# A two-layer encoder on one core: when banks are read, zeros behind the first transposes, where the last chunks are scaled, and who sums the MLP's weights

## The chip, the cores and the metric

The kernel runs on one core of one Trainium2 chip. The metric is the device time of one execution in microseconds (us). TensorE (PE) multiplies and writes PSUM banks; VectorE (DVE) and ScalarE (ACT) read those banks and work on tiles in SBUF; GpSimd (POOL) and SyncE (SP) issue the DMAs. PEld is PE's loading of weights, which overlaps its products.

## The reference

```python
for l in range(DEPTH):                       # 2 layers, x: 512 tokens by 1024
    h = _rmsnorm(x, g_mix[l])
    x = x + _mixer(h, l, w_in[l], ...)       # three attentions, three gates, one output projection
    h = _rmsnorm(x, g_mlp[l])
    x = x + jnp.square(jax.nn.relu(h @ w_up[l])) @ w_down[l]    # 1024 -> 4096 -> 1024
return _rmsnorm(x, g_final)
```

Inside the mixer one attention is dilated: a query sees keys of a window, and the scores of the group with dilation 1 are masked, their maximum is subtracted, and they are exponentiated.

## The kernel before

Everything is float32. A product is made of three matmuls: each operand is split into a high part (ACT copies it rounded) and a low part (DVE subtracts the high part from the original), and high times high, high times low and low times high are summed in a PSUM bank. Activations stand with features on the partitions and the 512 tokens along the row.

**A plan in place of written order.** Each line of the kernel only records an operation (`record`, line 184). `record` finds what it must wait for: for each tile read, the earlier writes that touch the same region (line 212), and for each tile written, earlier reads and writes. `schedule` (line 318) then walks through a model of time. Each engine takes, of the operations that are ready, the one recorded first (`key`), if its tiles fit in the slots; `cost` (line 247) gives durations, `bank_free` (line 473) keeps a bank from two engines at once, `try_alloc` (line 392) gives out tiles, and the DMA queues of POOL and SP are held to a backlog. At most 12 tiles `w` (cut weights) and 6 tiles `raw` (loaded weights) are alive, which sets how far the cutting can run ahead of the products. `emit` (line 598) writes the instructions out in the planned order, all from line 607, so that the profile shows L607 for nearly all of them; the tile names tell them apart. On the chip each engine runs its own list in order.

**The start** (from line 671). PE multiplies a tile of zeros six times (`warm`) while x is loaded. Then PE transposes x in eight blocks `k` of four 128x128 pieces into banks `x0` (shown as `x`), and DVE and ACT split each into `h`. The first products `mm<-w,h` follow.

**Scores** (`dil_scores`, line 1340). For the first group, two halves `i` of a bank `sp` (tile `s`) get two matmuls each, and then DVE reads each half with the mask, and writes `p0` (tile `pd`) and its maximum (`sm`):

```python
sp = P("s", [128, 2, 256])
for i in range(2):
    ten.matmul(sp[:, i], ..., kk[:, 0, w], start=True, stop=False)
    ten.matmul(sp[:, i], ..., kk[:, 1, w], start=False, stop=True)
for i in range(2):
    dve.tensor_tensor_reduce(p0[:, c], sp[:, i], mask0[...], ..., accum_out=ml0[:, c, 0:1])
```

There are four such units in a layer, of two banks each.

**The MLP** (label `mlp`). Nine of 16 pairs of up blocks (`up_pair`, line 1703, the numbers in `UP`) and all down blocks but the last (`down`, line 1743) use seven products in place of eight, in the way of Strassen and Winograd. `weights` (line 1668) loads four quarters a11, a21, a12, a22 of a weight block and makes seven cut operands of them, four of which are sums: s1 = a21 + a22, s2 = s1 - a11, a21 - a11, and a12 - s2 (tile `ss`, 128x512, or 128x384 where a group has three pairs). A set of these operands feeds 84 matmuls of 256 columns (63 with three pairs). There are 25 sets in a layer. Groups of 3, 4, 4 and 3 pairs (`PAIRS`) run one after the other: first the ups of the group, then its four downs, whose seven products `keep` (line 1754) adds up over the groups in DRAM by DMAs `da<-da` on POOL's queue, and `outputs` (line 1781) puts together at the end of the last group. On POOL the DMAs `da` each wait for ACT's copy of a bank. The seven products of a down block lie by pairs in banks (`BANKS`).

The last two pairs of ups, 14 and 15, have no Strassen form. Their squares `b` are split into `u` (`hilo`), multiplied with the last rows of w_down, and the result in the bank is multiplied by R2, the square of the norm's factor per token, into a tile `t`, and added to x (`xt`). In the last layer the columns 768 to 1023 are done in two halves of the tokens, then squared, summed and normed, transposed and written out.

Of the kernel before, what the change touches and what calls it, by code (L numbers as in the profile page):

```python
# [101 lines left out]
class Plan:  # L102
# [81 lines left out]
    def record(self, eng, m, args, kw):  # L184
# [23 lines left out]
        for v in reads:  # L208
            r = self.region(v)
            b = v.buf  # L210
            for w, wr in b.writes:
                if hit(wr, r):
                    preds.add(w.i)
            b.reads.append((op, r))
            if b not in op.bufs:
                op.bufs.append(b)
# [30 lines left out]
    def cost(self, eng, m, args, kw, reads, writes):  # L247
# [7 lines left out]
        if "dma" in m:  # L255
# [31 lines left out]
            return 900 if eng == "gpsimd" else 475 if k <= 256 else 600, lat  # L287
        n = free(o)
        psum = any(isinstance(v, View) and v.buf.space == "P" for v in reads)
        if m == "transpose":  # L290
# [27 lines left out]
    def schedule(self):  # L318
# [73 lines left out]
        def try_alloc(op):  # L392
# [19 lines left out]
            for b in new:  # L412
                if op.eng == "gpsimd" and o["lifo"]:

# [62 lines left out]
        while nleft:  # L477
# [9 lines left out]
            for e in engs:  # L487
                pe_, av_ = pend[e], avail[e]
                while pe_ and pe_[0][0] <= t:
                    i = heapq.heappop(pe_)[1]  # L490
                    heapq.heappush(av_, (ops[i].key, i))
                if free_t[e] > t or not av_ or e == "gpsimd" and flow_left() > o["backlog"]:
                    continue
                skipped = []
                pick = None
                while av_ and len(skipped) < 40:
                    c = heapq.heappop(av_)
                    w = bank_free(ops[c[1]])
                    if w > t:
                        heapq.heappush(pe_, (w, c[1]))  # L500
                        continue
                    if try_alloc(ops[c[1]]):
                        pick = ops[c[1]]
                        break
                    skipped.append(c)
# [12 lines left out]
                for b in op.bufs:  # L518
                    if b.users[-1] is op and b.words > 8 and b.cls:
                        u = [x for x in b.users if not done[x.i]]  # L520
                        if u:
# [3 lines left out]
                            if u[-1].i not in alloc_seen(evs, u[-1].i):  # L525
                                bisect.insort(evs, u[-1].i)
                if e in dmaq:
                    inq += op.lat
# [92 lines left out]
def trunk(ctx, tc, x, w_in, b_gate, g_mix, diff_lambda, g_diff, g_cq, g_ckv, w_uq, w_ukv,  # L621
# [6 lines left out]
    dr = ctx.enter_context(tc.tile_pool(name="dr", bufs=1, space=DRAM))  # L628
    opts = dict(n2=12, n4=42, limits=dict(x0=8, mm=5, s=3, tp=2, av=2, raw=6, w=12, p=8, pd=4, pt=4), boost=20, vecs=14e3, warm=6, backlog=6000, slack=150, late=120, dmalat=-750, dslack=3000, entry=300, begin=dict(gpsimd=1075, sync=560), lifo=1, ahead=dict(xt=300, raw=350, tb=300))
    plan = Plan(nc, sb, ps, x, {8: 64, 512: opts["n2"], 1024: opts["n4"]}, opts)  # L630
# [42 lines left out]
    dve.memset(zero, 0.0)  # L673
    p = P("mm")
    for _ in range(opts["warm"]):
        ten.matmul(p[:, :128], zero[:, :128], zero[:, :128], start=True, stop=True)
    mark("")
# [166 lines left out]
    for k in range(KD):  # L844
# [3 lines left out]
        norm.split(k, p)  # L848
        ps0.append(p)
    plan.boost = -opts["late"]  # L850
    for k in range(0, KD, 2):
# [35 lines left out]
    def layer(l, norm):  # L887
# [780 lines left out]
        def weights(w, k0, n, c0):  # L1668
# [15 lines left out]
            p1 = cut(a11)  # L1684
            s1 = add(dve.tensor_add, a21, a22)
            s2 = add(dve.tensor_sub, s1, a11)
            p6 = cut(s2)
            p7 = cut(add(dve.tensor_sub, a21, a11))
            p5 = cut(s1)
# [124 lines left out]
        for n in range(first, 16):  # L1814
            b = up_pair(n)
            for i in range(2):
                u = H("u")
                hilo(u, b[:, i].rearrange("p t n -> p (t n)"))
                us.append(u)
# [8 lines left out]
        for mp in range(4):  # L1828
# [6 lines left out]
            for i in range(2):  # L1835
                m = 2 * mp + i
                t = T("t")
                dve.tensor_mul(t, pp[i], R2)
                dve.tensor_add(xt[m], xt[m], t)
                if last:  # L1840
# [12 lines left out]
        for hh in range(2):  # L1853
# [5 lines left out]
            for i in range(2):  # L1859
                xm = xt[6 + i][:, cs]  # L1860
                t = T("t")
                dve.tensor_mul(t[:, cs], pp[i], R2[:, cs])
                dve.tensor_add(xm, xm, t[:, cs])
                sq = T("t")
# [81 lines left out]
```

## Time and profile before

| | us |
|---|---|
| median of 3 runs | 1913.08 (1911.11 to 1913.43) |
| the profiled execution | 1911.94 |
| its span in the trace | 1910.1 |
| PE busy | 1884.4 (99%) |
| DVE busy | 1547.6 (81%) |
| ACT busy | 1050.9 (55%) |
| POOL busy | 138.3 (7%) |

PE is at work nearly always, so the profile is read by PE's waits and by what stands ahead of them on the engine that ends them. The busy shares are averages over stages: in the attention of either layer DVE is busy for 71 to 87% of the time, in the first two thirds of the MLP for over 90%.

### The profile page before, as it was taken

How to read it: one execution, taken by the hardware profiler on the slowest of the kernel's cores; microseconds unless marked ns; L12 is line 12 of the kernel's file. 1: busy time of each engine (PE TensorE's matmuls, PEld its weight loads, DVE VectorE, ACT ScalarE, POOL GpSimd, SP SyncE). 2: the span in 40 equal slices, each digit the busy share in tenths (PEclk: the TensorE clock that was granted, in tenths of full speed). 3: DMA queues.
4: the chain of work that ended last, by engine and by line, in shares of the span. 5: the costliest groups of instructions: out<-in, count | busy, mean ns of one | idle time of the engine just before them, and what ended most of it. 6: DMA issues, size and time to landing. Idle time of an engine off the chain costs nothing.

```text
span 1910.1 us, 31918 instructions
## 1 busy us (share of the span) xinstructions
PE 1884.4 (99%) x11908; PEld 1685.5 (88%) x11908; DVE 1547.6 (81%) x3347; ACT 1050.9 (55%) x2029; POOL 138.3 (7%) x174
## 2 busy tenths in 40 slices
PE   9999999999999999999999999999999999999998
PEld 8888888887888999999988888888877889999997
DVE  7788867787788998958867988687877789989496
ACT  5564645544345776755444755455434467677544
POOL 0000001100110001010100000011001100010000
PEclk9999999999999999999999999999999999999999
DMA  8934636667562457592557364366766535384741
GB/s 221 235 100 129 187 116 187 175 166 228 155 176 79 130 169 162 137 268 91 165 125 196 84 201 143 111 166 174 185 188 174 160 102 183 108 201 120 218 144 50
DMA packets 273844, 301.33 MB, mean 158 GB/s; under 512 B 99789, under 2 KB 218573, under 8 KB 273689
## 3 DMA queue, kind: packets, MB, share of 16 engines
q1 hardware_dynamic: 250136, 214.74, 39.6%
q0 software_dynamic: 23552, 84.55, 16.5%
q8 instruction: 94, 1.54, 0.3%
q14 instruction: 62, 0.50, 0.1%
HBM read 222.36 MB, written 72.69 MB: 154 GB/s over the span
## 4 chain that ended last, share of the span: by engine, by line
PE 79%; DVE 10%; issue 6%; ACT 2%; DMA 2%; SPq 0%; POOL 0%; DVEq 0%; ACTq 0%; POOLq 0%
PE mm L607 53%; PE x L607 15%; PE s L607 4%; PE tp L607 4%; PE av L607 3%; DVE w L607 3%; ACT w L607 1%; DVE da L607 1%; DVE hb L607 1%; DVE ss L607 1%; DVE sm L607 1%; DVE t L607 1%; DVE ht L607 1%; DMA dk<-rx 1%; DMA ml<-sm 1%
## 5 line engine op out<-in xcount | busy, mean ns | idle before, releaser
L607 PE MATMUL mm<-h,w 128*128 128x512 f32 x2400 | 604.9, 397 | 2.0 <-DVE w L607 2.0
L607 PEld LDWEIGHTS mm<-h,w 128*128 128x128 f32 x2400 | 439.8, 188 | 94.5 <-DVE w L607 3.2
L607 PE MATMUL x<-u,w 128*128 128x256 f32 x3864 | 461.4, 281 | 4.7 <-ACT w L607 3.1
L607 PEld LDWEIGHTS x<-u,w 128*128 128x128 f32 x3864 | 458.1, 189 | 7.7 <-ACT w L607 3.7
L607 DVE TENSOR_TENSOR w<-raw,w 128x512 fp32r<-128x512 f32 (+3 forms) x432 | 356.3, 841 | 65.3 <-ACT w L607 63.7
L607 ACT ACTIVATE w<-raw 128x512 fp32r<-128x512 f32 (+3 forms) x432 | 309.8, 749 | 35.2 <-PE x L607 10.3
L607 PE MATMUL mm<-u,w 128*128 128x256 f32 (+1 forms) x1560 | 206.0, 294 | 0.1
L607 PEld LDWEIGHTS mm<-u,w 128*128 128x128 f32 x1560 | 197.3, 189 | 7.8 <-ACT w L607 0.5
L607 PE MATMUL mm<-w,h 128*128 128x256 f32 (+1 forms) x1152 | 153.5, 286 | 0.0
L607 PEld LDWEIGHTS mm<-w,h 128*128 128x128 f32 x1152 | 147.3, 190 | 2.4 <-DVE w L607 0.2
L607 ACT ACTIVATE w<-ss 128x512 fp32r<-128x512 f32 (+1 forms) x200 | 114.8, 592 | 58.7 <-DVE ss L607 40.0
L607 DVE TENSOR_TENSOR w<-ss,w 128x512 fp32r<-128x512 f32 (+1 forms) x200 | 125.1, 646 | 13.3 <-ACT w L607 12.8
L607 POOL DMA_DIRECT2D raw<-in_w_in_dram x80 | 70.1, 878 | 883.4 <-PE mm L607 236.9
L607 ACT ACTIVATE p<-s,sm 128x512 f32<-128x512 f32 x128 | 87.3, 684 | 84.7 <-DVE sm L607 83.8
L607 PE MATMUL s<-qk,qk 96*128 96x512 f32 (+2 forms) x448 | 120.7, 365 | 4.3 <-DVE sm L607 4.3
L607 PE MATMUL mm<-co,w 128*128 128x512 f32 x456 | 114.4, 398 | 0.1
L607 ACT ACTIVATE pt<-tp 128x512 fp32r<-128x512 f32 x128 | 70.9, 595 | 70.1 <-PE tp L607 69.1
L607 DVE TENSOR_REDUCE sm<-s 128x1 f32<-128x512 f32 x128 | 85.5, 682 | 21.0 <-PE s L607 20.8
L607 PEld LDWEIGHTS mm<-co,w 128*128 128x128 f32 x456 | 83.9, 188 | 19.0 <-DVE co L607 0.5
L607 DVE TENSOR_TENSOR t<-mm,const 128x512 f32<-128x512 f32 (+1 forms) x98 | 64.3, 674 | 43.7 <-PE mm L607 43.6
L607 PE MATMUL mm<-om,w 128*128 128x512 f32 x384 | 99.4, 396 | 0.0
L607 PEld LDWEIGHTS s<-qk,qk 128*128 128x128 f32 (+1 forms) x448 | 79.4, 189 | 19.1 <-DVE sm L607 5.2
(164 smaller groups left out, 2330.2 us busy)
## 6 DMA issues: line engine op xcount, KB each, us to landing
raw<-in_w_in_dram POOLq DMA_DIRECT2D x77, 512.0 KB, 7.2
raw<-in_w_up_dram SPq DMA_DIRECT2D x64, 512.0 KB, 5.7
dk<-rx SPq DMA_DIRECT2D x40, 512.0 KB, 6.4
qk<-dk SPq DMA_DIRECT2D x40, 512.0 KB, 5.4
raw<-in_w_down_dram SPq DMA_DIRECT2D x32, 512.0 KB, 4.4
raw<-in_w_in_dram SPq DMA_DIRECT2D x27, 512.0 KB, 9.9
raw<-in_w_down_dram SPq DMA_DIRECT2D x32, 384.0 KB, 3.9
da<-da POOLq DMA_DIRECT2D x24, 512.0 KB, 7.3
```

The source lines that it names most:

```text
L607: getattr(getattr(self.nc, op.eng), op.m)(*args, **kw)
```

## The change

- `record`: a read of a PSUM bank waits for every write recorded for that bank so far, not only for those that touch what is read.
- `weights`: the sums a21 + a22 and a21 - a11 are made by POOL, and recorded ahead of the other two. `cost` has a duration for such a POOL operation, and `try_alloc`, the backlog and the entry into the queue apply to POOL's DMAs alone.
- The start: eight zeros in place of six, and twelve more behind the transposes of the second block, with a piece of x as the weights, into the bank `idle` that nothing reads.
- The last two ups: `b` is multiplied by R2 before it is split, and the products are added to x straight from the bank, in the three places where a multiplication by R2 stood.

```diff
-                if hit(wr, r):
+                if hit(wr, r) or b.space == "P":
                     preds.add(w.i)
...
+        if eng == "gpsimd":
+            return 2.1 * n + 200, 300
...
-                if op.eng == "gpsimd" and o["lifo"]:
+                if op.eng == "gpsimd" and o["lifo"] and "dma" in op.m:
...
-                if free_t[e] > t or not av_ or e == "gpsimd" and flow_left() > o["backlog"]:
+                if free_t[e] > t or not av_:
                     continue
+                full = e == "gpsimd" and flow_left() > o["backlog"]
...
+                    if full and "dma" in ops[c[1]].m:
+                        skipped.append(c)
+                        continue
...
-                if e in dmaq:
+                if "dma" in op.m:
...
-    p = P("mm")
-    for _ in range(opts["warm"]):
-        ten.matmul(p[:, :128], zero[:, :128], zero[:, :128], start=True, stop=True)
+    idle = P("mm")
+
+    def zeros(n, w):
+        for _ in range(n):
+            ten.matmul(idle[:, :128], w, zero[:, :128], start=True, stop=True)
+    zeros(opts["warm"], zero[:, :128])
...
+        if k == 1:
+            zeros(opts["fill"], xin[0][:, 0, :128])
...
-            s1 = add(dve.tensor_add, a21, a22)
+            s1 = add(plan.gpsimd.tensor_add, a21, a22)
+            s3 = add(plan.gpsimd.tensor_sub, a21, a11)
             s2 = add(dve.tensor_sub, s1, a11)
             p6 = cut(s2)
-            p7 = cut(add(dve.tensor_sub, a21, a11))
+            p7 = cut(s3)
...
-                u = H("u")
-                hilo(u, b[:, i].rearrange("p t n -> p (t n)"))
+                u, t = H("u"), b[:, i].rearrange("p t n -> p (t n)")
+                dve.tensor_mul(t, t, R2)
+                hilo(u, t)
...
-                t = T("t")
-                dve.tensor_mul(t, pp[i], R2)
-                dve.tensor_add(xt[m], xt[m], t)
+                dve.tensor_add(xt[m], xt[m], pp[i])
```

(In the options, `warm` is 8 in place of 6, and `fill=12` is new. In the last layer's half columns the same replacement stands as in the last hunk.)

On PE the order is the same in both kernels from the end of the start to the scores of a dilated unit in layer 0 (at 465 us in the trace). There the bank of scores (`s_5424`, in the changed kernel `s_5438`) gets its four products among those of a gate (`mm_5385`, `mm_5399`). Before:

```order
L607 MATMUL s_5424<-qk_5272,qk_5241 128x256
L607 MATMUL mm_5385<-h_312,w_5139 128x512
L607 MATMUL s_5424<-qk_5272,qk_5241 128x256
L607 MATMUL mm_5385<-h_312,w_5152 128x512
L607 MATMUL s_5424<-qk_5272,qk_5241 128x256
L607 MATMUL mm_5385<-h_338,w_5139 128x512 x2
L607 MATMUL mm_5385<-h_338,w_5152 128x512
L607 MATMUL s_5424<-qk_5272,qk_5241 128x256
L607 MATMUL mm_5385<-h_347,w_5139 128x512 x2
```

Now:

```order
L613 MATMUL s_5438<-qk_5286,qk_5255 128x256
L613 MATMUL mm_5399<-h_326,w_5153 128x512
L613 MATMUL s_5438<-qk_5286,qk_5255 128x256
L613 MATMUL mm_5399<-h_326,w_5166 128x512
L613 MATMUL s_5438<-qk_5286,qk_5255 128x256
L613 MATMUL mm_5399<-h_352,w_5153 128x512
L613 MATMUL s_5438<-qk_5286,qk_5255 128x256
L613 MATMUL mm_5399<-h_352,w_5153 128x512
L613 MATMUL mm_5399<-h_352,w_5166 128x512
```

The fourth product `s` has moved up by two matmuls; in layer 1 the same row moves in the same way. DVE's reads of that bank stand at the same place in its list.

On DVE, at the end of the last group's downs in layer 0, the sums `ss` stand between the additions of `keep` (`da<-da,x`) and `outputs` (`hb`, `da<-da`), which end the downs, and the cuts `w` of the next set. Before:

```order
L607 TENSOR_TENSOR ss_10590<-raw_10343,raw_10353 128x384
L607 TENSOR_TENSOR da_9981<-da_9981,x_2015_10519 128x512
L607 TENSOR_TENSOR da_9981<-da_9981,x_2016_10522 128x256
L607 TENSOR_TENSOR hb_10610<-da_9927,da_9981 128x256 x2
L607 TENSOR_TENSOR hb_10610<-da_9927 128x256
L607 TENSOR_TENSOR da_9927<-da_9927 128x256
L607 TENSOR_TENSOR ss_10624<-ss_10590,raw_10343 128x384
L607 TENSOR_TENSOR hb_10610<-da_9927,da_9981 128x256
L607 TENSOR_TENSOR ss_10629<-raw_10343 128x384
L607 TENSOR_TENSOR w_10627<-ss_10624,w_10627 128x384
L607 TENSOR_TENSOR w_10598<-ss_10590,w_10598 128x384
```

Now:

```order
L613 TENSOR_TENSOR ss_10614<-ss_10433,raw_10357 128x384
L613 TENSOR_TENSOR da_9979<-da_9979,x_2017_10537 128x512
L613 TENSOR_TENSOR da_9979<-da_9979,x_2018_10540 128x256
L613 TENSOR_TENSOR hb_10634<-da_9927,da_9979 128x256 x2
L613 TENSOR_TENSOR hb_10634<-da_9927 128x256
L613 TENSOR_TENSOR da_9927<-da_9927 128x256
L613 TENSOR_TENSOR w_10622<-ss_10614,w_10622 128x384
L613 TENSOR_TENSOR hb_10634<-da_9927,da_9979 128x256
L613 TENSOR_TENSOR w_10501<-ss_10411,w_10501 128x384
L613 TENSOR_TENSOR w_10508<-ss_10433,w_10508 128x384
```

The sum of a21 and a22 (`ss<-raw,raw`) and the difference a21 - a11 (`ss<-raw`) have left DVE, and s2 (`ss<-ss,raw`) stands ahead of the additions.

On POOL, in the downs of the first group, nothing but the DMAs `da` stood before:

```order
L607 DMA da_1024_116<-da_7365 128x1024
L607 DMA da_768_117<-da_7339 128x768
L607 DMA da_1024_118<-da_7404 128x1024
L607 DMA da_768_119<-da_7450 128x768
L607 DMA da_1024_120<-da_7496 128x1024
L607 DMA da_768_121<-da_7561 128x768
```

Now:

```order
L613 DMA da_1024_116<-da_7370 128x1024
L613 DMA da_768_117<-da_7352 128x768
L613 TENSOR_TENSOR ss_7430<-raw_7343 128x512
L613 DMA da_1024_118<-da_7412 128x1024
L613 TENSOR_TENSOR ss_7481<-raw_7343,raw_7394 128x512
L613 DMA da_768_119<-da_7466 128x768
L613 TENSOR_TENSOR ss_7543<-raw_7440 128x512
L613 DMA da_1024_120<-da_7512 128x1024
L613 DMA da_768_121<-da_7577 128x768
L613 TENSOR_TENSOR ss_7612<-raw_7440,raw_7518 128x512
```

The sums for the next sets stand between the DMAs `da`, two to a set. From the second group on the list goes on in this way.

## Rows read from the trace of the kernel before

**Rows 1.** The page, part 1: busy us (share of the span) xinstructions by engine.
```profile
PE 1884.4 (99%) x11908; PEld 1685.5 (88%) x11908; DVE 1547.6 (81%) x3347; ACT 1050.9 (55%) x2029; POOL 138.3 (7%) x174
```

**Rows 2.** PE's waits in the whole run: us in total, times, longest.
```profile
PE s L607 <- DVE sm L607: 4.3, 2, 2.2
PE x L607 <- ACT w L607: 3.1, 3, 1.3
...
PE tp L607 <- DVE pd L607: 1.3, 1, 1.3
PE x L607 <- DVE w L607: 0.8, 2, 0.4
...
PE x L607 <- DVE u L607: 0.5, 2, 0.3
```

**Rows 3.** Timeline: start, us, engine, line, op, out<-in, xcount [idle before <-releaser].
```profile
466.46 1.22 DVE L607 TENSOR_TENSOR w<-raw,w 128x1024 fp32r<-128x1024 f32 x1
...
467.67 0.42 DVE L607 CUSTOM_DVE_ANT_0 pd<-s,const 128x256 f32<-128x256 f32 x1
...
468.15 0.39 PE L607 MATMUL s<-qk,qk 128*128 128x256 f32 x1 [2.14 <-DVE sm L607]
...
468.38 6.41 PE L607 MATMUL mm<-h,w 128*128 128x512 f32 x27
```

**Rows 4.** Windows, layer 0: busy PE, PEld, DVE, ACT, POOL; then `ss`: DVE, ACT.
```profile
640.00:665.00 25.00, 25.00 (x214) 24.86 (x213) 24.94 (x61) 17.39 (x33) 1.13 (x3) 1.00 0.39 119
665.00:725.00 60.00, 59.42 (x501) 58.99 (x500) 57.80 (x102) 45.21 (x86) 3.23 (x6) 1.00 0.47 153
725.00:760.00 35.00, 34.93 (x296) 34.94 (x297) 28.67 (x48) 22.91 (x42) 6.04 (x7) 1.00 0.88 195
760.00:815.00 55.00, 55.00 (x469) 54.89 (x469) 54.70 (x94) 41.31 (x75) 1.80 (x3) 1.00 0.56 145
...
640.00:665.00 25.00, 12.24 (x24) 4.36 (x9) 1.00 0.39 119
665.00:725.00 60.00, 28.15 (x45) 13.96 (x25) 1.00 0.47 153
725.00:760.00 35.00, 20.98 (x33) 9.47 (x16) 1.00 0.88 195
760.00:815.00 55.00, 24.21 (x38) 12.10 (x21) 1.00 0.56 145
```

**Rows 5.** Timeline of PE at the start.
```profile
1.49 2.93 PE L607 MATMUL mm<-t 128*128 128x128 f32 x12 [1.49 <-DVE t L607]
5.98 1.94 PE L607 MATMUL x<-const,v 128*128 128x128 f32 x8 [1.56 <-DMA v<-in_x_dram]
9.11 1.97 PE L607 MATMUL x<-const,v 128*128 128x128 f32 x8 [1.19 <-DMA v<-in_x_dram]
10.73 4.43 PE L607 MATMUL mm<-w,h 128*128 128x288 f32 x20
14.99 1.03 PE L607 MATMUL x<-const,v 128*128 128x128 f32 x8
```

**Rows 6.** DVE's sums of weights by form: xcount | busy us, mean ns | idle before.
```profile
L607 DVE TENSOR_TENSOR ss<-raw,raw 128x512 f32<-128x512 f32 x34 | 23.4, 688 | 0.0
...
L607 DVE TENSOR_TENSOR ss<-raw,raw 128x384 f32<-128x384 f32 x16 | 8.8, 553 | 0.0
```

**Rows 7.** Timeline of DVE at the end, and of PE at the layers' border.
```profile
1899.81 0.41 DVE L607 TENSOR_TENSOR t<-mm,const 128x256 f32<-128x256 f32 x1
...
972.76 0.43 PE L607 MATMUL tp<-const,const 128*128 128x128 f32 x2 [0.44 <-DVE const L607]
```

**Rows 8.** POOL: one form of instruction; timeline of POOL and DVE at 732 us.
```profile
masks.py:199 POOL TENSOR_SCALAR_AFFINE_SELECT const<-const 128x128 f32<-128x128 f32 x1 | 0.3, 287 | 0.1
...
732.22 1.78 POOL L607 DMA_DIRECT2D da<-da  x2 [50.04 <-ACT da L607]
...
733.23 1.29 DVE L607 TENSOR_TENSOR w<-ss,w 128x512 fp32r<-128x512 f32 x2 [1.07 <-ACT w L607]
```

More of the change, by code (lines that the diff above doesn't have):

```diff
@@ L628, in trunk @@
     dr = ctx.enter_context(tc.tile_pool(name="dr", bufs=1, space=DRAM))
-    opts = dict(n2=12, n4=42, limits=dict(x0=8, mm=5, s=3, tp=2, av=2, raw=6, w=12, p=8, pd=4, pt=4), boost=20, vecs=14e3, warm=6, backlog=6000, slack=150, late=120, dmalat=-750, dslack=3000, entry=300, begin=dict(gpsimd=1075, sync=560), lifo=1, ahead=dict(xt=300, raw=350, tb=300))
+    opts = dict(n2=12, n4=42, limits=dict(x0=8, mm=5, s=3, tp=2, av=2, raw=6, w=12, p=8, pd=4, pt=4), boost=20, vecs=14e3, warm=8, fill=12, backlog=6000, slack=150, late=120, dmalat=-750, dslack=3000, entry=300, begin=dict(gpsimd=1075, sync=560), lifo=1, ahead=dict(xt=300, raw=350, tb=300))
     plan = Plan(nc, sb, ps, x, {8: 64, 512: opts["n2"], 1024: opts["n4"]}, opts)
@@ L1860, in layer @@
                 xm = xt[6 + i][:, cs]
-                t = T("t")
-                dve.tensor_mul(t[:, cs], pp[i], R2[:, cs])
-                dve.tensor_add(xm, xm, t[:, cs])
+                dve.tensor_add(xm, xm, pp[i])
                 sq = T("t")
```

## The prediction

> **What bounds the kernel now.** I read the page's busy times first: TensorE (PE) is busy for 1884.4 of 1910.1 us [rows 1]. No edit here takes a product away (the zeros add some), so nothing can be won but PE's waits and the two ends, some 25 us together. The second view is the list of what PE waited for [rows 2]. Its longest entry is 4.3 us in two waits of a matmul `s` for VectorE (DVE). The waits of `x` products, those of the MLP, for freshly cut weights or halves come to 3.1 + 0.8 + 0.5 = 4.4 us. The third view is the stall at 465 us, one of the two [rows 3]. PE writes the two halves of a bank of scores with four products `s`, and DVE may read half 0 as soon as the first two are done. That read (467.67) stands in DVE's queue behind a weight cut of 1.22 us (466.46), and PE's fourth product waits 2.14 us for it, since both touch one bank. The fourth view is the layer 0 MLP by stretches [rows 4]. In 640-665, 665-725 and 760-815 us DVE is busy for 24.94 of 25, 57.80 of 60 and 54.70 of 55 us while PE hardly waits; only 725-760 leaves it 6.3 us. So in the MLP DVE runs level with PE, and each microsecond put on DVE there is paid by PE.
>
> **Banks read whole.** In `record` a read of a bank now follows every product written to it so far. Only in the first loop of `dil_scores` are a bank's halves read one by one, so nothing else can move, and up to the MLP the order confirms it: apart from the start, one row moves in each layer, the fourth `s` product, two matmuls up. DVE's place for the reads stays. What PE waited for is gone, because the read is now behind the product. What is late next: 27 products `mm` follow the stall without a wait [rows 3], on weights cut before it. Gain 4.3 us, both layers. Cost: the read of half 0 now waits for two products more, but it starts 2 us behind them anyway: nothing. Bounds 2.2 (one stall comes back elsewhere) to 4.3; I take 4.3, the row itself.
>
> **Zeros at the start.** PE waits for x until 5.98 us, again until 9.11 [rows 5]. Eight transposes take 1.94 us there and 1.03 at 14.99, so the early ones run at the lower of the clock's two levels, though the column PEclk has no sign of it. Two more zeros in front end before 5.98: free. Twelve zeros between the first and the second block take twice the records of the first row each, 24 by 2.93/12 = 5.9 us at the lower level, half of it at the higher. They start at about 7.7. At the lower level throughout they end at 13.6; then come the transposes of 9.11, 1.0 us at the higher level, and the first 20 products, some 2.6 (a little over half of their 4.43, since the last of them ran fast already): 17.2 instead of 15.2, 2.0 lost. At the higher level from their start, they end at 10.6, and 1.0 and 2.6 more make 14.2: 0.9 won. Which it is depends on when the clock rises, and that no row of before tells. I take 0.5 lost, nearer to the middle.
>
> **Last chunks scaled first.** Removed: eight multiplications `t<-mm` per layer; added: four in SBUF on `b`, 0.69 us each like other rows of that shape [rows 6]. On the path to the end stands one: DVE multiplies for 0.41 us at 1899.81, adds behind it, and ScalarE (ACT) squares behind that [rows 7]. The sum goes straight from the bank now, so the end comes 0.4 us sooner; where the other `t<-mm` of 0.41 counts too, 0.8. At the layers' border the chain to the norm loses a multiplication of 0.69, and PE's wait of 0.44 there [rows 7] can go: 0.4. On the other side, the new multiplication stands between the square and the split of the last up pair, 0.7 us on a chain that ends shortly before PE needs it: 0.1 lost, cover DVE idle there. Together 0.7 won.
>
> **Two sums by GpSimd (POOL).** 25 sets of weights per layer, two sums each: DVE loses 34 + 16 rows of either kind, 0.688 or 0.553 us [rows 6]; two of 0.69 in a row take 1.29 (733.23, rows 8), so 0.60 is what one gives back, in the small form 0.46. POOL gets 100 sums. It has no tensor sum before; the nearest row that reads SBUF is a select over 128 elements, 0.287 us [rows 8], so a sum of 512 takes up to 1.15 us, of 384 up to 0.86 (an estimate). POOL is 93% idle, and one set feeds 84 products, 84 by 60/501 us = 10 us of PE [rows 4], so its own length is covered by a set's lead. POOL's queue is in order: sums now stand between the DMAs `da`, which wait for ACT (732.22, rows 8). A sum behind such a DMA waits with it; behind the sum wait DVE's second sum (and all that DVE has queued behind that) and ACT's cuts, and then PE. The set's lead of 10 us is the cover; where it is used up, PE waits for what is left of the `da` wait.
>
> The price that decides is what DVE loses while POOL reads SBUF beside it. The rows bound it from 0 to the whole sum, 1.15. For 0 speaks that DVE's cuts keep 0.69 while POOL issues DMAs for 1.78 us (733.23 beside 732.22, rows 8); but such an issue reads no tile, so that is the nearest row, not a near one. At 0 DVE is 0.60 ahead per sum, and nearly all of the 4.4 us of `x` waits go [rows 2], the longest two of 1.3 too: there DVE's second sum stood behind additions for the outputs, and in the new order stands ahead of them. I put 4.0 on it. At 0.60 the sum is even and nothing is won. I take the middle of these two, 2.0 won: some of the sums must fall beside DVE's reads of PSUM or its waits for ACT, and up to 0.6 of 1.15 costs nothing.
>
> The Trainium skill speaks against this edit. "SBUF — State Buffer", section "Who interferes with whom", states that a VectorE instruction with two inputs in SBUF contends with a GpSimd instruction that reads SBUF, and that whichever issues second stands still until the other is done. No row here shows such a pair. By that rule the whole sum would be lost, and the time would be that of the first rival below.
>
> **Sum**, against the profiled execution of 1911.94 us (span 1910.1): 4.3 won, 0.5 lost, 0.7 won, 2.0 won = 6.5 won: 1905.4. The median of the runs is 1.1 above that execution, by which it is 1906.6; I say 1906. With all bounds, the forecast's own range is 4.3 + 0.9 + 1.2 + 4.0 = 10.4 won to 4.3 - 2.0 + 0.7 = 3.0 won: 1901 to 1910.
>
> **Rivals.** *POOL's sums hold DVE* (slower). Each sum costs DVE 1.15 and gives back 0.60 (0.86 and 0.46). The sets in a stretch are the instructions on `ss` by eight [rows 4]: six small sums in 640-665, 11 in 665-725, 8 in 725-760, 9.5 in 760-815. Over DVE's idle time that is 6 by 0.40 = 2.4; 11 by 0.55 less 2.2 = 3.9; 8 by 0.55 less 6.3 = nothing; 9.5 by 0.55 less 0.3 = 4.9. So PE loses 11.2 us per layer, 22.4 in all, against 4.5 won elsewhere: 1913.1 + 17.9 = 1931. It decides from about 0.87 us lost per sum, where 11 by 0.27 - 2.2, 9.5 by 0.27 - 0.3 and 6 by 0.19 come to 4.2 per layer, and the whole is 3.8 slower. For it: DVE's instructions there nearly all read two tiles. Against it: DVE's waits for ACT and its PSUM reads take part of a sum.
>
> *The gain moves on* (same). The stalls of `s` go, but one of them comes back at the next late chain, `tp` waiting for `pd` (1.3 us already [rows 2]), whose DMAs need not move with PE; the zeros cost their 2.0, POOL's sums come out even: 4.3 - 2.2 - 2.0 + 0.7 = 0.8 won: 1912. This is also the case in which the first edit doesn't do what it says.
>
> **How the numbers follow.** 0.2% (3.8 us) is about what a measurement of this kernel can tell from no change. Forecast 0.52, of it 0.04 within 0.2%; POOL holds DVE 0.30, of it 0.04 within; moved gain 0.18, of it 0.03 faster, 0.01 slower. So faster 0.51, same 0.22, slower 0.27. The range reaches from the forecast's best, 1901, into the first rival, to 1925: about 0.05 is left out below, 0.12 above, the full price of that rival among it.
>
> **What would show it.** No wait of `s` for DVE in PE's list: the first step. PE's first 20 products starting before 12 us or after 14: the zeros. `xt<-xt,mm` directly ahead of the last square, and the end 0.4 us nearer: the scaling. POOL's sums at about 1.1 us, and DVE's cuts beside them at 0.69: the forecast; cuts of over 1 us and PE waits for `w` in the MLP of more than 5 us per layer: the first rival. I am wrong if DVE's instructions stretch beside POOL's sums by more than 0.6 each, or if the sums come late behind the `da` DMAs.

## The result, and the profile after

The changed kernel takes 1959.92 us (median of 4 runs, 1955.38 to 1960.51) against 1912.09 us before in the same session: a ratio of 1.0237, with an interval from 1.0225 to 1.025. I had forecast 1906 and a range of 1901 to 1925. It is 47.8 us slower (43 to 48 by the interval), beyond the full price that I gave to the first rival.

Part 1 of the page of the changed kernel:

```profile
PE 1907.9 (97%) x11936; PEld 1703.6 (87%) x11936; DVE 1575.1 (80%) x3237; ACT 1049.5 (54%) x2029; POOL 317.1 (16%) x274
```

Against [rows 1], DVE has 110 instructions fewer and is busy 27.5 us longer. So its other instructions got longer. POOL is busy for 178.8 us more, with 100 instructions more. PE has 28 more (14 zeros, two records each), and is busy 23.5 us longer; 24.3 us more of the span (50.0 instead of 25.7) is idle. The loss has these two halves.

PE's waits in the whole run of the changed kernel (us in total, times, longest):

```profile
PE x L613 <- DVE u L613: 15.2, 10, 3.2
PE x L613 <- ACT u L613: 12.5, 14, 2.5
PE tp L613 <- DVE sm L613: 5.0, 3, 2.5
PE x L613 <- DVE w L613: 3.8, 7, 0.9
```

The entry `s` for DVE, the longest of [rows 2], is gone, as the first step wanted. New are 27.7 us of waits of the MLP's products for `u`, the split halves. Weights `w`, which the first rival named, are only 3.8. New as well are two waits of `tp` for `sm` of 2.46 and 2.36 us (at 647.68 and 1613.28 us), in the norm ahead of the MLP: there DVE's small instructions on `sm`, 0.16 us alone, take up to 0.98 us beside a sum.

In the list of all waits of the changed kernel, none of PE, DVE or ACT is put down to a sum by POOL. The sums a21 + a22, taken in order, are done 1.1 us or more before DVE takes them up, in the median 11 us. So the sums do not come late.

The layer 0 MLP by stretches (us; busy PE, PEld, DVE, ACT, POOL with counts; granted clock, DMA share, GB/s):

```profile
640.00:665.00 25.00, 22.30 (x173) 21.70 (x172) 22.95 (x49) 14.93 (x28) 5.57 (x6) 0.93 0.30 88
665.00:725.00 60.00, 59.06 (x494) 58.45 (x493) 55.44 (x78) 39.48 (x79) 24.36 (x18) 1.00 0.51 165
725.00:760.00 35.00, 28.06 (x194) 26.74 (x193) 28.74 (x41) 20.52 (x36) 15.78 (x10) 0.80 0.45 100
760.00:815.00 55.00, 55.00 (x468) 55.00 (x467) 47.98 (x63) 33.93 (x63) 20.63 (x16) 1.00 0.76 179
815.00:835.00 20.00, 15.64 (x93) 14.14 (x92) 19.48 (x34) 13.08 (x22) 13.94 (x2) 0.74 0.16 52
```

In 665-725 DVE works almost as long as in [rows 4] (55.4 and 57.8 us), but finishes 78 instructions there instead of 102. In 725-760 PE is idle for 6.9 us, and its granted clock is 0.80 on average: after those waits it stood at the lower of its two levels, 1.2 GHz, for part of the stretch. Each of the three stretches here with more than 2 us of waits has such a drop (0.93, 0.80, 0.74).

Who was stretched: the groups of DVE and POOL by form (xcount | busy us, mean ns | idle before).

```profile
L613 POOL TENSOR_TENSOR ss<-raw 128x512 f32<-128x512 f32 x34 | 78.2, 2299 | 209.8 <-DMA raw<-in_w_up_dram 102.8 <-DMA raw<-in_w_down_dram 55.5 <-ACT w L613 29.4
L613 POOL TENSOR_TENSOR ss<-raw,raw 128x512 f32<-128x512 f32 x34 | 63.4, 1864 | 28.8 <-DMA raw<-in_w_down_dram 14.2 <-DMA raw<-in_w_up_dram 10.9 <-DVE w L613 3.3
...
L613 DVE TENSOR_TENSOR w<-raw,w 128x512 fp32r<-128x512 f32 x230 | 175.6, 783 | 30.0 <-ACT w L613 29.2
L613 DVE TENSOR_TENSOR w<-ss,w 128x512 fp32r<-128x512 f32 x136 | 100.4, 760 | 15.1 <-ACT w L613 14.3
...
L613 DVE TENSOR_TENSOR ht<-x,t 128x512 f32<-128x512 f32 x18 | 12.3, 681 | 0.5 <-PE x L613 0.5
```

A sum of 512 elements takes POOL 2.30 and 1.86 us on average; the shortest took 1.28 (of 384 elements: 1.00). DVE's cuts of 512, 0.69 before, are at 0.78 and 0.76 over all. `ht<-x,t` has one input in PSUM (`x` is a bank), and keeps its 0.68.

I went through the trace for every DVE instruction that overlaps one of POOL's sums, and set each against the median of the same form where none runs:

```
changed kernel, DVE form          alone: n, mean    beside a sum: n, mean
w<-raw,w 512 (SBUF, SBUF)        193, 0.68 us       37, 1.30 us
w<-ss,w  512 (SBUF, SBUF)        104, 0.69 us       32, 1.00 us
acc<-acc,t 512 (SBUF, SBUF)       39, 0.69 us        4, 1.78 us
ht<-x,t  512 (PSUM, SBUF)         11, 0.68 us        7, 0.68 us
all forms: 83.8 us lost on DVE beside the 100 sums
```

In all, 19 DVE instructions with an input in PSUM ran beside a sum; each took 0.67 to 0.69 us. So 0.84 us are lost per sum, and only instructions whose inputs all lie in SBUF lose them. This is what the Trainium skill states ("SBUF — State Buffer", section "Who interferes with whom"): a VectorE instruction with two inputs in SBUF contends with a GpSimd instruction that reads SBUF. The trace agrees (1.30 against 0.68 us for the first of these forms).

How this reaches PE is to be seen at 730 us (start, us, engine, line, op, out<-in, xcount [idle before <-releaser]):

```profile
729.86 1.72 POOL L613 TENSOR_TENSOR ss<-raw 128x512 f32<-128x512 f32 x1
730.38 2.28 DVE L613 TENSOR_TENSOR u<-ht,u 128x1024 fp32r<-128x1024 f32 x1
731.54 2.27 POOL L613 TENSOR_TENSOR ss<-raw,raw 128x512 f32<-128x512 f32 x1
732.59 0.68 DVE L613 TENSOR_TENSOR ht<-x,ht 128x512 f32<-128x512 f32 x1
732.72 2.72 PE L613 MATMUL x<-u,w 128*128 128x256 f32 x11 [2.71 <-DVE u L613]
...
735.33 1.93 ACT L613 ACTIVATE hb<-hb 128x768 f32<-128x768 f32 x2 [5.18 <-DVE hb L613]
...
737.30 0.94 ACT L613 ACTIVATE u<-hb 128x512 fp32r<-128x512 f32 x2
...
737.98 0.58 PE L613 MATMUL x<-u,w 128*128 128x256 f32 x1 [2.54 <-ACT u L613]
```

The split of the halves, `u<-ht,u`, takes 2.28 us instead of 1.22, because POOL's sums run through it; PE's next product waits 2.71 us for it. Behind the split stand on DVE the sums that make the next halves (`ht<-x,ht` at 732.59 and two on `hb`). So ACT's squares of them are late, having waited 5.18 us for DVE, then ACT's split at 737.30, and PE waits again until 737.98. It is one chain: products, halves, split, products.

Such a place is where the loss is paid, but not only where it arises. The run below in which POOL writes zeros has the same order on PE, DVE and ACT, so that the two can be set against each other instruction by instruction. At 710 us DVE is 12.6 us behind that run, and PE, working on what was cut ahead, only 5.2. At 745 us PE is 17.7 behind, DVE 16.5. Then it goes the same way again: at 815 us DVE is 26.4 behind and PE still 17.7, at 835 us PE is 26.9 behind. From 815.87 to 833 us none of DVE's instructions is stretched, and PE waits six times all the same.

### The profile page after: what moved, and what is told of

Read it like the earlier page. It is cut to its first block, busy times and chain, and to the rows that moved or that the text cites. A ratio compares the mean times of both kernels' runs of the same rounds, so it can differ in the third digit from the quotient of the medians.

```text
span 1957.9 us, 32160 instructions
## 1 busy us (share of the span) xinstructions
PE 1907.9 (97%) x11936; PEld 1703.6 (87%) x11936; DVE 1575.1 (80%) x3237; ACT 1049.5 (54%) x2029; POOL 317.1 (16%) x274
## 4 chain that ended last, share of the span: by engine, by line
PE 76%; DVE 16%; issue 4%; ACT 2%; DMA 1%; DVEq 0%; POOL 0%; SPq 0%; ACTq 0%; POOLq 0%
PE mm L613 56%; PE x L613 10%; DVE w L613 5%; PE s L613 4%; PE tp L613 4%; PE av L613 3%; DVE ht L613 2%; DVE u L613 2%; DVE ss L613 2%; DVE hb L613 1%; DVE sm L613 1%; DVE da L613 1%; ACT w L613 1%; ACT hb L613 1%; DMA fs<-t 0%
## 5 line engine op out<-in xcount | busy, mean ns | idle before, releaser
L613 PE MATMUL x<-u,w 128*128 128x256 f32 x3864 | 482.9, 287 | 31.9 <-DVE u L613 15.2
L613 PEld LDWEIGHTS x<-u,w 128*128 128x128 f32 x3864 | 473.5, 194 | 40.8 <-DVE u L613 18.5
L613 DVE TENSOR_TENSOR w<-raw,w 128x512 fp32r<-128x512 f32 (+3 forms) x432 | 384.3, 906 | 76.4 <-ACT w L613 74.6
L613 ACT ACTIVATE w<-raw 128x512 fp32r<-128x512 f32 (+3 forms) x432 | 311.2, 749 | 42.7 <-PE x L613 11.5
L613 DVE TENSOR_TENSOR w<-ss,w 128x512 fp32r<-128x512 f32 (+1 forms) x200 | 144.0, 738 | 18.6 <-ACT w L613 17.5
L613 POOL TENSOR_TENSOR ss<-raw 128x512 f32<-128x512 f32 (+1 forms) x50 | 97.2, 1944 | 311.9 <-DMA raw<-in_w_up_dram 102.8
L613 PE MATMUL av<-pt,v 128*128 128x256 f32 x576 | 94.4, 288 | 0.0
```

What stands on the lines that cost most here:

```text
L613: getattr(getattr(self.nc, op.eng), op.m)(*args, **kw)
```

## The experiments

Three theories stand behind the expectations. **H**: POOL's sums hold DVE, and DVE them, as the first rival has it. **L**: the sums come late behind other work in POOL's queue. **O**: the loss is in the other edits, or in the order that the planner makes of them. **S**, for a sum put down earlier, was formed after the first four runs. The times of before beside each group are 1912.42, 1913.13 and 1913.56 us.

**All of the change, but the sums on DVE.**

```diff
-            s1 = add(plan.gpsimd.tensor_add, a21, a22)
-            s3 = add(plan.gpsimd.tensor_sub, a21, a11)
+            s1 = add(dve.tensor_add, a21, a22)
+            s3 = add(dve.tensor_sub, a21, a11)
```

> All of the change except the two sums by GpSimd: VectorE makes all four. Theory H (GpSimd's sums hold VectorE, and VectorE them): the loss goes altogether, and what is left is the rest of the forecast's sum, 4.3 - 0.5 + 0.7 = 4.5 us won: 1906 to 1911. Theory L (the sums come late behind other work in GpSimd's queue): the same, 1906 to 1911. Theory O (the other edits, or the new order that the planner makes of them, lose the time): 1935 or more.

Measured: 1931.58 us, ratio 1.01 (1.0085 to 1.0115). None of the theories had this: 28 us of the loss go with POOL's sums, but the rest of the change is not faster than before, it is 19 us slower. DVE's cuts have their old length, and PE waits 6.2 us for ACT's `u`, 5.9 for ACT's and 5.5 for DVE's `w`.

**The changed kernel's order, the sums issued to DVE.** The plan is made as in the changed kernel; only the engine is swapped when the instructions are written out.

```diff
+            eng = "vector" if op.eng == "gpsimd" and op.m in ("tensor_add", "tensor_sub") else op.eng
-            getattr(getattr(self.nc, op.eng), op.m)(*args, **kw)
+            getattr(getattr(self.nc, eng), op.m)(*args, **kw)
```

> The order of the changed kernel, instruction for instruction, but the 100 sums are issued to VectorE, at their places in time, instead of GpSimd. VectorE gets back 100 instructions, some 60 us of work, in an order that was made without them. Theory H: faster than the changed kernel all the same, since 0.84 us lost per sum is more than the 0.60 that one takes: 1910 to 1930, TensorE at the full clock throughout. Theory L: 1906 to 1920. Theory O (the order is at fault): 1955 or more, as the changed kernel or slower.

Measured: 1933.21 us, ratio 1.011 (1.0093 to 1.0127), a little above the upper end of H. With 100 instructions more on DVE, in an order made without them, the kernel is 27 us faster than with POOL doing them. The full clock throughout, which was expected too, did not come: 0.994 on average, with 13.2 us of waits for ACT's `u`.

**The changed kernel's order, POOL writing zeros in place of the sums.**

```diff
+            if op.eng == "gpsimd" and op.m in ("tensor_add", "tensor_sub"):
+                self.nc.gpsimd.memset(args[0], 0.0)
+            else:
                 getattr(getattr(self.nc, op.eng), op.m)(*args, **kw)
```

> The order of the changed kernel, but in place of each of the 100 sums GpSimd writes zeros to the same tile, so it reads nothing from SBUF; two of the four sums are left out of the result. GpSimd's queue, its places and who waits for its tiles stay; only the wait for the weights' load goes. Theory H: no VectorE instruction is stretched (cuts of 512 at 0.69 throughout), and the forecast comes true, 1903 to 1909. Theory L: the tiles still come behind the transfers da, so at least half of the loss stays: 1930 or more. Theory O: 1955.

Measured: 1903.07 us, ratio 0.9951 (0.9936 to 0.9966). H's number, and L's and O's are out of reach. The groups of POOL and DVE by form, and the three largest of PE's waits in the MLP:

```profile
L614 POOL MEMSET ss<- 128x512 f32 x68 | 39.4, 598 | 157.1 <-DVE w L616 37.3 <-DVE co L616 31.4 <-DVE ht L616 26.6
...
L616 DVE TENSOR_TENSOR w<-raw,w 128x512 fp32r<-128x512 f32 x230 | 153.0, 684 | 35.3 <-ACT w L616 32.5 <-DMA qk<-dq 1.9
```

```profile
PE x L616 <- DVE w L616: 1.8, 2, 0.9
PE x L616 <- ACT u L616: 1.3, 2, 0.9
...
PE x L616 <- DVE u L616: 0.4, 2, 0.2
```

The cuts are back at 0.68, and by the count of overlaps DVE loses less than 0.1 us in all beside 100 writes. The order that carries 1959.9 with sums carries 1903.1 with writes. A write also needs no load of weights and is shorter than a sum, so the next run and the one with copies were needed as well.

**The kernel before, with 100 spare sums that nobody reads.**

```diff
             getattr(getattr(self.nc, op.eng), op.m)(*args, **kw)
+            if op.spare:      # s1 and the sum for p7, which DVE makes as before
+                v = spare[:, :128 * n].rearrange("p (j n) -> p j n", n=128)
+                getattr(self.nc.gpsimd, op.m)(v, args[1], args[2])
```

> The kernel before in its own order, VectorE making all four sums; beside it GpSimd makes the same 100 sums into a spare tile that nobody reads. Theory H: VectorE loses some 0.84 us per sum, 84 us in all, with nothing given back, and the MLP has little idle time of it to take them: 1955 to 2000, VectorE's two-tile instructions beside the sums at over 1.2 us instead of 0.69. Theory L: nobody waits for these sums, so 1911 to 1917. Theory O: 1911 to 1917.

Measured: 1986.14 us, ratio 1.0385 (1.0369 to 1.04). Nobody reads these sums, PE, DVE and ACT keep their order, and 74 us are lost. The groups of POOL and DVE by form, and the longest waits of PE for `w` and of ACT for what the sums hold up:

```profile
L616 POOL TENSOR_TENSOR spare<-raw,raw 128x512 f32<-128x512 f32 x34 | 122.1, 3590 | 144.7 <-DMA raw<-in_w_down_dram 78.2 <-DMA raw<-in_w_up_dram 66.0
...
L610 DVE TENSOR_TENSOR w<-ss,w 128x512 fp32r<-128x512 f32 x136 | 115.8, 871 | 16.2 <-ACT w L610 16.0
```

```profile
PE x L610 <- DVE w L610: 27.1, 31, 2.2
...
ACT w L610 <- POOL spare L616: 17.4, 5, 4.2
...
ACT w L610 <- DMA raw<-in_w_up_dram: 16.3, 6, 3.8
PE x L610 <- ACT w L610: 16.3, 7, 4.9
```

DVE loses 92.0 us beside them, 0.92 per sum. Here PE does wait for `w`, as the rival said. The run does not by itself leave L out, though nobody reads the sums: five of ACT's cuts wait 17.4 us for a spare sum, and six wait 16.3 us for loads of w_up (before: none of either). One spare sum took 23.46 us. So part of the 74 us may have come in this way. What speaks against L in the changed kernel is its own list of waits, with none for a sum and one of 1.0 us for a load of the MLP's weights.

**The kernel before with the first three edits.** Banks, zeros and scaling, and its own four sums by DVE.

```diff
-                if hit(wr, r):
+                if hit(wr, r) or b.space == "P":
...
-opts = dict(... warm=6, ...)
+opts = dict(... warm=8, fill=12, ...)
...
-                t = T("t")
-                dve.tensor_mul(t, pp[i], R2)
-                dve.tensor_add(xt[m], xt[m], t)
+                dve.tensor_add(xt[m], xt[m], pp[i])
```

> The kernel before with the first three edits (banks read whole, zeros at the start, last chunks scaled first) and its own four sums in their own places; GpSimd makes none. In the MLP VectorE's order is that of the kernel before, up to its last chunks. Theory H (the sums by GpSimd and what goes with them are the whole loss): the terms of the forecast without the sums, 1906 to 1910. Theory O, now narrowed: if one of these three edits costs what the first run showed (the change without GpSimd's sums took 1931.6), 1925 or more.

Measured: 1903.96 us, ratio 0.9952 (0.9937 to 0.9966), faster than both kernels and 2 us better than the terms of the forecast. So none of the three edits made the 19 us of the first run. What is left between the two is the line that puts down the second sum ahead of `s2` and its cut, which no term of the prediction names. PE's waits and its start:

```profile
PE x L607 <- ACT w L607: 3.4, 3, 1.3
...
PE x L607 <- DVE w L607: 0.8, 2, 0.4
PE x L607 <- DVE u L607: 0.5, 2, 0.3
```

```profile
5.89 1.06 PE L607 MATMUL x<-const,v 128*128 128x128 f32 x8 [0.94 <-DMA v<-in_x_dram]
6.79 2.84 PE L607 MATMUL mm<-t,v 128*128 128x128 f32 x24
9.47 1.04 PE L607 MATMUL x<-const,v 128*128 128x128 f32 x8
10.27 2.89 PE L607 MATMUL mm<-w,h 128*128 128x288 f32 x20
```

**The kernel before with that one line moved.**

```diff
             s1 = add(dve.tensor_add, a21, a22)
+            s3 = add(dve.tensor_sub, a21, a11)
             s2 = add(dve.tensor_sub, s1, a11)
             p6 = cut(s2)
-            p7 = cut(add(dve.tensor_sub, a21, a11))
+            p7 = cut(s3)
```

> The kernel before with one line moved: the second of the two sums in question is put down ahead of the sum s2 and its cut, as the change does it for GpSimd, but VectorE still makes it. Nothing else is changed. Theory S (a sum put down earlier takes VectorE's time from cuts and halves that PE needs sooner, in an MLP where VectorE has no time to spare): this alone costs the 19 us of the first run and what the three edits win, 1928 to 1937. Theory O: 1911 to 1915.

Measured: 1938.88 us, ratio 1.0138 (1.0123 to 1.0153): 26 us for a line that adds no work. S stands, and a little more than priced. The new plan differs from that of before in 254 of DVE's places and 139 of ACT's, and in none of PE's. PE's waits for `w` and `u` grow from 4.4 to 18.8 us, and PE is busy for 11.5 us more, which no view here divides. One of the places where PE pays, in order of time:

```profile
812.35 0.68 DVE L607 TENSOR_TENSOR ss<-raw,raw 128x512 f32<-128x512 f32 x1
812.95 0.68 DVE L607 TENSOR_TENSOR ss<-raw 128x512 f32<-128x512 f32 x1
813.55 0.68 DVE L607 TENSOR_TENSOR ss<-ss,raw 128x512 f32<-128x512 f32 x1
...
813.66 0.63 ACT L607 ACTIVATE w<-ss 128x512 fp32r<-128x512 f32 x1 [2.91 <-DVE ss L607]
814.20 0.58 ACT L607 ACTIVATE hb<-mm 128x512 f32<-128x512 f32 x1
...
816.27 0.94 ACT L607 ACTIVATE u<-hb 128x512 fp32r<-128x512 f32 x2
...
816.96 7.22 PE L607 MATMUL x<-u,w 128*128 128x256 f32 x45 [2.81 <-ACT u L607]
```

Three sums stand in a row on DVE. ACT's next cut is that of the second of them, the sum that was moved, and waits 2.91 us until it is made (813.63); behind it on ACT stand the read of the bank, the square and the split of the halves, and PE waits 2.81 us for those. Neither DVE nor ACT has more to do than before. What stands ahead of what has changed. That the whole 26 us arise in this way is argued from such places, not shown.

**The sum by POOL, put down in its old place.**

```diff
-            s3 = add(plan.gpsimd.tensor_sub, a21, a11)
...
-            p7 = cut(s3)
+            p7 = cut(add(plan.gpsimd.tensor_sub, a21, a11))
```

> The changed kernel with the second sum, still by GpSimd, put down where it stood before, behind s2 and its cut. Theory H: GpSimd reads SBUF as long beside VectorE, so the loss stays: 1940 to 1970. If the new place were the fault on GpSimd too (Theory S for both engines): 1915 to 1935.

Measured: 1957.25 us, ratio 1.0229 (1.0214 to 1.0244). The planner made of it the same order as of the changed kernel on PE, DVE, ACT and POOL. So this was a second measurement of the changed kernel. With the sum on POOL the line's place means nothing to the plan; the 19 and 26 us above belong to DVE's order alone, and are no part of the changed kernel's loss.

**The changed kernel's order, POOL copying one tile in place of each sum.**

```diff
+            if op.eng == "gpsimd" and op.m in ("tensor_add", "tensor_sub"):
+                self.nc.gpsimd.tensor_copy(args[0], args[1])
+            else:
                 getattr(getattr(self.nc, op.eng), op.m)(*args, **kw)
```

> The order of the changed kernel, but GpSimd copies one of the two tiles in place of each of the 100 sums (one input from SBUF instead of two; two of the four sums are left out of the result). If any reading by GpSimd holds VectorE's two-tile instructions: they stretch again, in proportion to the copy's length, and the time lies at 1925 to 1960. If it takes a GpSimd instruction with two inputs: no stretch, 1902 to 1909, as with zeros written.

Measured: 1925.14 us, ratio 1.0067 (1.005 to 1.0084), the lower end of the first answer. The copies wait for the loads as the sums do; alone they take 0.61 us (512 elements) and 0.51 (384). DVE loses 36.7 us beside them. So one input is enough, and the loss goes with the length of the reading: 0.37 us per copy, 0.84 per sum, none per write.

**The three edits one by one, and the two front zeros alone.** The diffs are those of the three-edit kernel, one at a time; the last is `warm=6` to `warm=8` without `fill`.

> The kernel before with the first edit alone: a read of a bank follows every product written to it so far. The forecast's term: 4.3 us won, so 1908.8 against 1913.1; 1911 if one of the two stalls comes back elsewhere. If the wait of tp for pd at 1475 goes with it, as in the run of the three edits, 1.3 us more: 1907.5.

Measured: 1906.88 us, ratio 0.9968 (0.9956 to 0.9979): 6.7 us, between 4.0 and 8.4 by the interval, so the forecast's 4.3 is not excluded. The wait of `tp` for `pd` [rows 2] is gone from the list as well (it is gone too in the two runs below that have only zeros, so it does not hang on this edit alone).

> The kernel before with two more zeros in front and twelve behind the second block of transposes. By the forecast's term 0.5 us lost, 1913.6; by the start of the three-edit run, where the next products began 2.0 us sooner, 1911. No other engine's work changes, so what is won at 15 us should still be there at the end.

Measured: 1912.43 us, ratio 0.9999 (0.999 to 1.0008). At the start the 2.0 us are there (the third eight transposes begin at 13.03 instead of 14.99 [rows 5]; in other profiled executions with the old start they begin between 14.21 and 14.79), at the end they are not. The stretches around the first stall of `s` show where part of them went in the profiled execution:

```profile
465.00:468.00 3.00, 1.57 (x4) 1.37 (x5) 1.97 (x7) 1.38 (x5) 0.27 (x1) 0.71 0.99 280
468.00:469.00 1.00, 1.00 (x4) 0.72 (x3) 0.68 (x1) 0.81 (x4) 0.41 (x1) 0.50 1.02 414
469.00:472.00 3.00, 3.00 (x13) 2.46 (x12) 1.31 (x3) 1.76 (x3) 0.35 (x1) 0.89 1.04 334
```

Behind the stall of 2.2 us the granted clock falls to its lower level for a while, which by these rows costs 3 by 0.29 + 0.50 + 3 by 0.11 = 1.7 us. In the profiled execution of before the same stall is followed by 1.00 throughout. So such a stall sometimes costs its own 2.2 us and sometimes 1.7 more. Whether the first edit's 6.7 us hold some of this is open: between the profiled executions of before and of that run, neither with a drop at this place, the difference is 6.5 us, 4.3 of it the wait of `s` and 1.3 that of `tp`. The whole time cannot tell 2 us: its interval alone is 3.4 us wide.

> The kernel before with the last chunks scaled first, alone. The forecast's term: 0.7 us won (0.4 at the end, 0.4 at the layers' border, 0.1 lost before the last up pair), 1912.4; from the gaps of the three-edit run, 0.3 at the end and 0.4 at the border. Any loss of over 1 us would fall on the multiplications that now stand in front of the splits of the last up pairs.

Measured: 1913.95 us, ratio 1.0005 (0.9996 to 1.0013): nothing that can be measured. PE's wait of 0.44 at the border [rows 7] is gone, in this run and in the three-edit one. By their medians the three edits alone won 6.7, 1.1 and -0.4 us, 7.4 in all, where the three together won 9.2; the intervals do not tell these apart.

> The kernel before with two more zeros in front and none behind the transposes. If the two in front alone bring TensorE's higher clock sooner: the first eight transposes take 1.0 us instead of 1.94, and the products behind them are back by under 1.5 us. If the clock needs TensorE to be kept busy through the wait for the second block as well: the second eight still take near 1.97, and nothing is won at 15 us: 1912.5 to 1913.5.

Measured: 1912.81 us, ratio 0.9999 (0.999 to 1.0007). PE at the start:

```profile
5.90 1.06 PE L607 MATMUL x<-const,v 128*128 128x128 f32 x8 [0.86 <-DMA v<-in_x_dram]
8.77 1.97 PE L607 MATMUL x<-const,v 128*128 128x128 f32 x8 [1.80 <-DMA v<-in_x_dram]
10.39 3.40 PE L607 MATMUL mm<-w,h 128*128 128x288 f32 x20
```

Each answer is half right. The first eight run at the higher level already (1.06 instead of 1.94), the second eight, after a wait of 1.80, at the lower one again (1.97). The third eight still begin at 13.62, sooner than with the old start. The twelve behind the first block are what holds the clock: with them the second eight take 1.04 and the 20 products 2.9 instead of 3.4.

## Why the prediction was wrong

**Banks read whole** (4.3 won): right in kind and place, both stalls are gone in every kernel with this edit. Alone it won 6.7 (4.0 to 8.4 by its interval), so the size is not contradicted either. The next late chain, `tp` for `pd`, did not take a stall over, as the second rival feared.

**Zeros** (0.5 lost, from 0.9 won to 2.0 lost): the bounds were right in kind, the clock having two answers, but the better one was put too low. In the three-edit run the two front zeros bring the higher level before x is there, the 24 records take 2.84 us from 6.79, and the third eight transposes start at 12.99: 2.0 won against [rows 5]. I had let the 24 start at 7.7, behind transposes that are slow. In the profiled execution of the changed kernel the clock came later, and it is 0.4 lost, near the 0.5 that I had put:

```profile
6.25 1.94 PE L613 MATMUL x<-const,v 128*128 128x128 f32 x8 [0.98 <-DMA v<-in_x_dram]
7.99 4.08 PE L613 MATMUL mm<-t,v 128*128 128x128 f32 x24
...
15.41 1.04 PE L613 MATMUL x<-const,v 128*128 128x128 f32 x8
```

So the same start goes either way: of the eight profiled executions that have it, six begin the third eight transposes at 12.93 to 13.37, two at 15.00 and 15.41. What decides it no run here shows, and that the changed kernel's execution came out near my 0.5 is luck.

**Last chunks scaled first** (0.7 won): within what cannot be measured; the border's 0.4 is there.

**Two sums by POOL** (2.0 won): this step failed. Against the three-edit kernel, which has all but the sums, the changed kernel loses 1959.9 - 1904.0 = 56 us. Both have 11936 matmuls, so the two spans divide it: PE is busy for 1907.9 instead of 1884.3 us, 23.6 longer, and idle for 32.5 us more. Some 15 of the 23.6 us are the clock. In five stretches of the changed kernel, 47.8 us together, the granted clock is 0.50, and PE is busy for 32.7 us of them, against 3.4 in the three-edit kernel; half of the difference is what the lower level cost. The other 9 no view here divides. The step had three parts.

- The price per sum, which I put midway between 0 and 0.60, the point where a sum comes out even. It is 0.84, beyond that point. I leaned on the row in which DVE's cuts run beside POOL's DMA issues at 0.69 [rows 8], and wrote that such an issue reads no tile. That was the difference that mattered: 100 writes cost DVE less than 0.1 us in all, 100 readings 37 to 92.
- What DVE's relief would bring, which I put at nearly all of 4.4 us. With POOL only writing, PE's waits for `w` and `u` come to 3.5 us, against 4.7 in the three-edit run. With some 50 us less work on DVE (busy 1493.3 instead of 1542.5 us) PE waited about 1.2 us less.
- How a loss on DVE reaches PE. I netted it: so much lost per sum, less 0.60 given back, over DVE's idle time. At 0.84 per sum that gives, by the first rival's working, a kernel some 2 us slower. What the runs show is close to the gross: 83.8 us of stretch cost 56.8 us against the run with writes, and 36.7 cost 22.1, so 0.60 to 0.68 us for each microsecond of stretch; with the spare sums (nothing given back) 92.0 cost 73.7, late loads included. What the sums gave back won almost nothing by itself, as the run with writes shows. The stretch gathers on DVE over a whole stretch of the MLP, and PE pays for it where it next needs split halves: from 726 to 745 us PE falls from 7.0 to 17.7 us behind the run with writes. And I left out what a wait costs beyond itself, the clock above all: each microsecond that PE was idle more cost 1.7 (56.1/32.5, against the three-edit run), with the spare sums 1.4 (PE busy 22.6 longer and idle 51.2 longer than before).

The **first rival** was thus the right mechanism with a total too low by 29 us, and 0.30 was too little a chance for it. Its 1.15 per sum was more than the 0.84 measured; too low was what PE pays, for it took off what the sums give back and all of DVE's idle time. The rule of the Trainium skill ("SBUF — State Buffer", section "Who interferes with whom"), which I had weighed, had the whole sum lost. Measured are 0.84 us of the 1.19 that a sum takes at its shortest (68 of 1.28 and 32 of 1.00). I set against it that DVE's waits and its reads of PSUM would take part of each sum; the 19 reads of PSUM do run free, but against 84 us that is little. My mark for this rival was PE waiting for `w`; in the changed kernel it waits for `u`.

**The moved line.** The change puts the second sum ahead of `s2`. I did not price it, and on POOL it changes nothing, since the plan comes out the same. But it means that the changed kernel cannot be mended by giving the sums back to DVE as they stand (1931.6): they have to go back to their places (1904.0).

## What to carry to other kernels

Before moving elementwise work from VectorE to GpSimd, look at what VectorE runs beside it: instructions with all inputs in SBUF lost 0.84 us for each GpSimd sum here, instructions that read PSUM lost nothing, and GpSimd instructions that only write cost nothing. Price such a loss gross, as VectorE falling behind until TensorE next needs its work, and not net against the work given back; and add what TensorE's clock loses behind the waits. And take a change of four edits apart: three of these make the fastest kernel of this study that computes the whole result.

## What the runs showed of the hardware that I had not expected

- The hold works both ways and not in turns. POOL sums that take 1.28 us at the shortest took up to 13.03 in the changed kernel, while DVE's instructions ran on one behind the other:

```profile
821.06 13.03 POOL L613 TENSOR_TENSOR ss<-raw 128x512 f32<-128x512 f32 x1 [9.27 <-ACT w L613]
```

- Even instructions on four elements are held: in the changed kernel five `sm<-sm` with one input and a scalar took 0.64 us on average beside a sum, 0.17 otherwise, and four with two tiles as inputs 0.96 to 0.99, 0.16 otherwise. So an instruction with one tile in SBUF as input can be held too.
- One stall of 2.2 us in a PE that is otherwise hardly idle is followed by the lower clock in some executions (0.50 in the run with zeros alone) and not in others (1.00 in before), which is worth 1.7 us each time.
